# A two-layer decoder trunk on one core: block differences of the feed-forward's activations formed on VectorE when they are made, and product 2 summed in four PSUM banks

## The chip, the cores and the metric

The kernel runs on one core of one Trainium2 chip. The metric is the device time of one execution in microseconds; lower is better. TensorE (PE) multiplies into PSUM, VectorE (DVE), ScalarE (ACT) and GpSimd (POOL) work on SBUF and PSUM, and SyncE (SP) issues the transfers. PSUM has eight banks of [128, 512] f32 here, which the kernel deals out to two pools, A of three and B of five.

## The reference

Two layers on x of 1024 tokens by 1024 features, f32. Layer 0 mixes tokens with gated linear attention, layer 1 with differential attention; each is followed by a SwiGLU feed-forward, and a norm ends it. What the change touches is the feed-forward:

```python
def swiglu(h, w_in, w_out):
    gate, up = jnp.split(h @ w_in, 2, axis=-1)
    return (jax.nn.silu(gate) * up) @ w_out

for i in range(DEPTH):
    ...  # mixer of the layer: x = x + Mixer(rmsnorm(x))
    x = x + swiglu(rmsnorm(x, norm_ffn[i]), ffn_w_in[i], ffn_w_out[i])
return rmsnorm(x, norm_final)
```

w_in is 1024 x 5632 (gate and up of 2816 hidden features, 22 hidden tiles of 128), w_out is 2816 x 1024.

## The kernel before

Everything is kept transposed: features on the partitions, tokens along a row. The residual stream is eight row tiles of two token halves, `xt[k][s]`, each [128, 512] f32. A product of full precision is three matmuls: each operand is split into a high part (a cast on ScalarE, L143) and a low part (source minus high part, a subtraction on VectorE, L144), and high x high, high x low and low x high are summed in one bank. `split` does this for activations and weights; a matmul has 128x128 weights and 512 columns.

`swiglu` is called once per layer. `a` and `b` are its first and second token half. In its **first stage** it makes the 22 hidden tiles. Tiles 0 and 1 are computed directly; beside them the second token half's norm is finished and the sums and differences of normed blocks are made (`norm_b`, `combos`; `whole`, L925, adds a high and a low part together again). All other tiles go in seven block products (`p1` to `p7`, 12 matmuls each; Winograd's form of a 2x2 block product), in the order 2 to 18, 20, 21, 19. `finish` multiplies the up part by the gate and writes the result, [128, 512] of one token half, to DRAM (`stash`).

In the **second stage** the output products run over five groups of four hidden tiles. A group's activations are a 2x2 of blocks: B11 and B21 are token half a of the group's first and second pair of tiles, B12 and B22 the same of token half b. Their combinations T1 = B12 - B11, T3 = B22 - B12, T2 = B22 - T1, T4 = B21 - T2 and the blocks B11, B22, B21 enter seven products for each of four row pairs (rows i and i + 4). `oprod` does one of them (six matmuls) and adds the bank to one tile of the residual stream on VectorE (L881). Products 1, 6, 7, 4 of a row pair sum in one bank ("u"), 5 and 3 in another ("v"), 2 in a third ("w"); u is taken from pool B, v and w from pool A. The order of the products is a sorted list that sets them a few places apart:

```python
at = {1: 0, 5: 1, 6: 3, 3: 4, 2: 5, 7: 6, 4: 9}
order = sorted((7 * (4 * g + i) + at[n], g, i, n) for g in range(NG - 1) for i in range(4) for n in at)
```

`stash_steps(g)` makes the 20 steps that bring a group's blocks back: four loads of 512 KB (L804), the four differences on GpSimd (L818, 128x1024), and 14 splits. They are spread evenly beside the 28 products of the group before. `chunk_load` loads a row pair's weights (L828, 512 KB) and forms their four sums on GpSimd (L832 to L835, 128x256); `chunk` splits them. The last two hidden tiles, 20 and 21, have output products of their own (`direct_outp`, added at L916), with weights from `direct_weights` (L888) and activations from `direct_acts` (L906).

The **junction** lies between the stages: beside the products of tile 19 the first group's blocks and the first weights are loaded, differenced and split, and `direct_outp` for half a follows. The Tile framework keeps the order in which the code is written on each engine except where `tc.issue_after` or a priority moves it, and sets the semaphores; a tile's buffer is reused when its last reader is done.

Of the kernel before, what the change touches and what calls it, by code (L numbers as in the profile page):

```python
# [8 lines left out]
F32 = mybir.dt.float32  # L9
# [7 lines left out]
P = 128  # L17
# [9 lines left out]
NW = 5  # L27
# [27 lines left out]
def trunk_kernel(ctx: ExitStack, tc: tile.TileContext, xT, gin, gv, ga, gb, gout,  # L55
# [56 lines left out]
    # weights: two raw tiles and NW split sets, taken in turn  # L112
# [72 lines left out]
    def squares(s, ks, acc=None, c=slice(0, HT)):  # L185
        """Squares of rows ks, summed (on top of acc)."""
# [40 lines left out]
    def first_weights(layer, s):  # L227
        """Gate and up weights of the layer's first hidden tile, where token half s has left its normed tokens."""
# [12 lines left out]
    # ================= layer 0: gated linear attention =================  # L241
    pcA = ExitStack()
    psum(pcA, ("A", 3), ("B", 5))
    with ExitStack() as pc:
# [3 lines left out]
        def work():  # L248
            """Scratch; while the other token half's normed input is idle, its slots serve too."""
# [14 lines left out]
        def load_gate():  # L264
            # ga holds the 16 columns twice: the second copy becomes their low part
# [12 lines left out]
        # The tokens of the first half enter the projections before their norm's scale is known: it is a factor of  # L278
        # each token, and the results take it.
# [131 lines left out]
        def unit_steps(u):  # L411
# [23 lines left out]
            def level(m):  # L435
# [160 lines left out]
        # in the order in which tokens and weights come in  # L596
# [43 lines left out]
    # ================= SwiGLU =================  # L640
    # gate and up products of a hidden tile in seven block products (Winograd's form; rows: gate, up; contraction
    # halves; columns: the token halves). The first two hidden tiles go directly: their products hide the norm of
    # the second token half and the combinations of its blocks.
    def swiglu(layer, gcol, first_w, last, first=0):
# [5 lines left out]
        with ExitStack() as pc:  # L650
# [62 lines left out]
            def prod(ps, f, wn, bn, cont=False):  # L713
                """Block product into a bank; cont: on top of what the bank holds."""
# [53 lines left out]

            def finish(f, s, up, gate):
                g, r = divmod(f, 4)  # L770
                e = ftile(f"e{c.setdefault('e', 0) % 4}")
                c["e"] += 1
# [6 lines left out]
            stash = [dram.tile([P, 4096], F32, name=f"stash{layer}_{g}") for g in range(NG + 1)]  # L779
            X, SB = {}, {}  # L780
# [598 lines left out]
```

## Time and profile before

| | |
|---|---|
| median of 3 runs | 2437.61 us (2436.07 to 2438.44) |
| span of the profiled execution | 2436.8 us; no other time of its own is recorded |
| first mixer, to about | 498 us |
| feed-forward of layer 0: first stage, junction, groups | 498 to 920, 920 to 966, 966 to 1145 us |
| second mixer, to about | 1762 us |
| feed-forward of layer 1: first stage, junction, groups | 1762 to 2165, 2165 to 2219, 2219 to 2398 us |

Busy time of an engine over the span says which engine could bound the kernel; the list of waits says for which tile of which engine an engine stood still; the table of windows gives busy time, granted TensorE clock and DMA share of chosen stretches. The stages' bounds were read from the timeline.

### The profile page before, as it was taken

The numbers are of one execution on the slowest core, as the hardware profiler recorded it, in microseconds if no ns is written. First come the engines' busy times: TensorE is split into PE (matmuls) and PEld (weight loads), VectorE is DVE, ScalarE is ACT, GpSimd is POOL, SyncE is SP. The second block draws the span as 40 slices with busy tenths as digits, with TensorE's granted clock in tenths as the row PEclk, the third lists the DMA queues.
The fourth block names the chain that finished last, engine by engine and source line by source line (L and its number), as shares of the span: only waits on it lengthen the run. The fifth ranks groups of instructions, "written<-read, shape, count | busy, mean of one in ns | idle before, by whom it ended". The sixth has DMA issues, their size and how long they took to land. (4 is left out here: it accounts for less than half of the span.)

```text
span 2436.8 us, 31021 instructions
## 1 busy us (share of the span) xinstructions
PE 2363.2 (97%) x11930; PEld 1958.5 (80%) x11930; DVE 1814.3 (74%) x2890; ACT 1077.0 (44%) x1741; POOL 374.3 (15%) x284
## 2 busy tenths in 40 slices
PE   8999999999999998999999999999899999999997
PEld 6888888877888887787788878787678888877876
DVE  7767765887666559999876675857886655679998
ACT  6445644534333334334565454646443333333334
POOL 4000000030000004773000000000220000025763
PEclk9999999999999999999999999999999999999999
DMA  5122222113222223332010101010023222234322
GB/s 188 61 70 70 70 78 78 53 44 112 79 86 85 89 78 121 107 108 98 27 35 18 36 18 40 31 36 29 18 65 101 88 89 78 78 100 128 101 87 87
DMA packets 59780, 180.68 MB, mean 74 GB/s; under 512 B 6640, under 2 KB 8816, under 8 KB 59632
## 3 DMA queue, kind: packets, MB, share of 16 engines
q1 hardware_dynamic: 59344, 178.55, 22.7%
q8 instruction: 94, 1.54, 0.3%
q14 instruction: 54, 0.44, 0.1%
q10 hardware_dynamic: 288, 0.16, 0.0%
HBM read 151.41 MB, written 27.26 MB: 73 GB/s over the span
## 5 line engine op out<-in xcount | busy, mean ns | idle before, releaser
L925 POOL TENSOR_TENSOR t4h<-hh,hl 128x512 f32<-128x512 f32 x8 | 13.9, 1754 | 1037.5 <-DVE hl L144 1037.5
L832 POOL TENSOR_TENSOR sums<-wraw 128x256 f32<-128x256 f32 x40 | 32.2, 806 | 846.0 <-PE psB L718 368.8
L144 DVE TENSOR_TENSOR w3h<-wraw,w3h 128x512 fp32r<-128x512 f32 x40 | 27.7, 692 | 161.1 <-ACT w3h L143 161.1
L144 DVE TENSOR_TENSOR w0l<-wraw,w0h 128x1024 fp32r<-128x1024 f32 (+2 forms) x60 | 67.9, 1132 | 90.3 <-ACT w0h L143 90.2
L1149 ACT ACTIVATE p<-sp,mx 128x128 f32<-128x128 f32 (+7 forms) x128 | 94.8, 743 | 78.5 <-DVE mx L1146 77.9
L881 DVE TENSOR_TENSOR x<-x,psB 128x512 f32<-128x512 f32 (+1 forms) x180 | 119.2, 665 | 9.6 <-PE psB L879 8.6
L717 PE MATMUL psB<-hh,w0h 128*128 128x512 f32 x320 | 124.7, 390 | 0.3 <-ACT rs L726 0.2
L719 PE MATMUL psB<-hh,w0l 128*128 128x512 f32 x320 | 124.6, 389 | 0.0
L718 PE MATMUL psB<-hl,w0h 128*128 128x512 f32 x320 | 124.5, 389 | 0.0
L1145 DVE TENSOR_REDUCE mx<-sp 128x1 f32<-128x128 f32 (+7 forms) x128 | 94.9, 753 | 39.0 <-PE sp L1143 37.8
L143 ACT CAST w0h<-wraw 128x1024 fp32r<-128x1024 f32 (+2 forms) x60 | 58.8, 980 | 128.6 <-PE psB L718 98.4
L143 ACT CAST w2h<-wraw 128x1024 fp32r<-128x1024 f32 (+2 forms) x58 | 56.9, 980 | 114.4 <-PE psB L718 92.4
L225 DVE TENSOR_TENSOR x<-x,psA 128x512 f32<-128x512 f32 x108 | 73.5, 684 | 37.8 <-PE psA L150 35.8
L143 ACT CAST w3h<-wraw 128x512 fp32r<-128x512 f32 x42 | 26.1, 621 | 149.5 <-DMA wraw<-in_fin 145.6
L1174 PE MATMUL psO<-aT,vd 128*128 128x128 f32 x576 | 80.6, 280 | 0.5 <-ACT aT L1170 0.4
L1174 PEld LDWEIGHTS psO<-aT,vd 128*128 128x128 f32 x576 | 72.7, 192 | 9.3 <-ACT aT L1170 7.2
L1140 PE MATMUL sp<-kk,qh 128*128 128x512 f32 (+2 forms) x192 | 73.7, 384 | 5.1 <-DVE kk L1098 3.2
L143 ACT CAST w1h<-wraw 128x1024 fp32r<-128x1024 f32 (+1 forms) x44 | 45.5, 1035 | 60.1 <-DVE wraw L689 49.2
L881 DVE TENSOR_TENSOR x<-x,psA 128x512 f32<-128x512 f32 x104 | 69.2, 675 | 3.1 <-PE psA L879 2.7
L717 PEld LDWEIGHTS psB<-hh,w0h 128*128 128x128 f32 x320 | 60.1, 188 | 13.5 <-ACT rs L726 1.2
L717 PE MATMUL psB<-t3h,w2h 128*128 128x512 f32 x160 | 63.9, 399 | 7.0 <-DVE sq L744 7.0
L719 PEld LDWEIGHTS psB<-hh,w0l 128*128 128x128 f32 x320 | 60.1, 188 | 12.8 <-DVE w0l L144 0.3
(666 smaller groups left out, 8106.4 us busy)
## 6 DMA issues: line engine op xcount, KB each, us to landing
wraw<-in_fin SPq DMA_DIRECT2D x88, 512.0 KB, 3.9
stash<-e SPq DMA_DIRECT2D x88, 256.0 KB, 2.6
wraw<-in_foutc SPq DMA_DIRECT2D x40, 512.0 KB, 3.7
wraw<-in_gin SPq DMA_DIRECT2D x32, 512.0 KB, 3.7
raw<-stash SPq DMA_DIRECT2D x20, 512.0 KB, 4.5
wraw<-in_gv SPq DMA_DIRECT2D x16, 512.0 KB, 3.6
wraw<-in_gout SPq DMA_DIRECT2D x16, 512.0 KB, 3.6
wraw<-in_din SPq DMA_DIRECT2D x16, 512.0 KB, 3.6
```

The costliest lines, as they stand in the source:

```text
L143: ins = nc.scalar.copy(out=hi, in_=src)
L144: nc.vector.tensor_tensor(out=lo, in0=src, in1=hi.bitcast(F32), op=ALU.subtract)
L225: nc.vector.tensor_tensor(out=xt[m][s], in0=xt[m][s], in1=ps, op=ALU.add)
L717: mm(ps, ah, bh, start=s, stop=False, skip_group_check=cont)
L718: mm(ps, ah, bl, start=False, stop=False, skip_group_check=cont)
L719: mm(ps, al, bh, start=False, stop=i == KH - 1, skip_group_check=cont)
L832: op(out=s1, in0=a21, in1=a22, op=ALU.add)
L881: tt(out=xt[i + o][s][:, c], in0=xt[i + o][s][:, c], in1=ps, op=ALU.add)
L1140: mm(out, qh[:, o:o + P], kk[:, :w], start=True, stop=False)
L1145: nc.vector.reduce_max(out=mx, in_=sp[:, :W], axis=AX.X)
L1149: nc.scalar.activation(out=p[:, :W], in_=sp[:, :W], func=AF.Exp, scale=scale, bias=mx, accum_out=sm)
L1174: mm(c["op"][:, o:o + P], tl["v", n // 2][:, j, v * P:(v + 1) * P], aT[:, j * P:(j + 1) * P], start=j == 0, stop=j == i)
```

## The change

`finish` no longer writes only the four blocks. As soon as an activation is made, it also forms T1, T3, T2 and T4 from it on VectorE ([128, 512] each, 40 per layer), and the stash of a group holds seven blocks, in 14 pieces of 256 KB. `stash_steps` loads these straight into the tiles of the low parts and splits them in place: 14 steps where there were 20. B11 of group 0 is loaded and split early, beside tile 19's first products. The sums of `whole` and all combinations of normed blocks move from GpSimd to VectorE, those for T4 behind product 1. The sums of the first two weight chunks move to VectorE, the others stay. Product 2 of all five groups sums in the banks that `direct_outp` of half a has begun for rows 0 to 3 (`WB`: the three banks of pool A and one of B) and is added to the residual stream once, in the last group; u and v of all row pairs take turns in the other four banks of pool B.

```diff
+            def etile():
+                c["e"] = c.get("e", -1) + 1
+                return ftile(f"e{c['e'] % 4}")
+
+            def keep(g, o, t):
+                nc.sync.dma_start(out=stash[g][:, o * HT:(o + 1) * HT], in_=t)
+
             def finish(f, s, up, gate):
+
+
                 g, r = divmod(f, 4)
...
+                j = r % 2
+                d = blk.setdefault((g, j), {})
+                if g < NG and r < 2 and s == b:
+                    if ("keep", g) not in blk:
+                        blk["keep", g] = ftile("raw0", 1024), ftile("raw1", 1024)
+                    d["B12"], d["T1"] = [t[:, j * HT:(j + 1) * HT] for t in blk["keep", g]]
+                    e = d["B12"]
+                else:
+                    e = etile()
                 tt(out=e, in0=up, in1=gate, op=ALU.mult)
-                o = (r // 2 * 2 + (s == b)) * 1024 + r % 2 * HT
-                nc.sync.dma_start(out=stash[g][:, o:o + HT], in_=e)
...
+                if g == NG:
+                    return keep(g, 2 * (s == b) + j, e)
+                put = lambda n, t: keep(g, 2 * NAMES.index(n) + j, t)
+                if s == a:
+                    d["ea"] = e
+                    put("B21" if r > 1 else "B11", e)
+                elif r < 2:
+                    tt(out=d["T1"], in0=e, in1=d["ea"], op=ALU.subtract)
+                    put("T1", d["T1"])
+                else:
+                    put("B22", e)
+                    tt(out=d["B12"], in0=e, in1=d["B12"], op=ALU.subtract)
+                    put("T3", d["B12"])
+                    t2, t4 = etile(), etile()
+                    tt(out=t2, in0=e, in1=d["T1"], op=ALU.subtract)
+                    put("T2", t2)
+                    tt(out=t4, in0=d["ea"], in1=t2, op=ALU.subtract)
+                    put("T4", t4)
...
+            stash = [dram.tile([P, 7168 if g < NG else 2048], F32, name=f"stash{layer}_{g}") for g in range(NG + 1)]
+            NAMES = ("B11", "T1", "T2", "B22", "B21", "T3", "T4")
+            X, SB, blk = {}, {}, {}
...
                 if g % 2 == 0:
-                    t = ht(range(2, KD), a) + ft((2, 3))
-                    order = ("B11", "T3", "T2", "B22", "T1", "B21", "T4")
+                    w4 = [wpool.tile([P, 1024], F32R, name=f"w4{x}") for x in "hl"]
+                    t = ([[t[:, o:o + HT] for o in (0, HT)] for t in w4] + ht(range(2, 4), a) + ft((2,)) + ht(range(4, KD), a) +
+                         ft((3,))[:2])
                 else:
                     t = ht(range(KD), b) + ft((4,)) + ht(range(2), a)
-                    order = ("T2", "T3", "T4", "T1", "B22", "B21", "B11")
-                return {n: t[2 * i:2 * i + 2] for i, n in enumerate(order)}
+                return {n: t[2 * i:2 * i + 2] for i, n in enumerate(NAMES)}
...
+
+                def load(names):
+                    X.setdefault(g, {})
+                    for n in names:
+                        X[g][n] = X["slots", g][n]
+                        for j in range(2):
+                            o = (2 * NAMES.index(n) + j) * HT
+                            nc.sync.dma_start(out=X[g][n][j][1].bitcast(F32), in_=stash[g][:, o:o + HT])
 
                 def sp(n, j):
                     def go():
-                        split(*X[g][n][j], R[n][:, j * HT:(j + 1) * HT])
+                        hi, lo = X[g][n][j]
+                        split(hi, lo, lo.bitcast(F32))
...
-                def comb(n, x, y):
-                    # the result takes the place of an operand that is not needed again
-                    dst = {"T1": "B11", "T3": "B12", "T2": "B22", "T4": "B21"}[n]
-                    sub(out=R[dst], in0=R[x], in1=R[y], op=ALU.subtract)
-                    R[n] = R[dst]
+                def slot():
...
                 sps = lambda n: [lambda j=j: sp(n, j) for j in range(2)]
-                return ([load] + sps("B11") + [lambda: comb("T1", "B12", "B11")] + sps("B22") +
-                        [lambda: comb("T3", "B22", "B12"), lambda: comb("T2", "B22", "T1")] + sps("T1") +
-                        sps("B21") + sps("T2") + [lambda: comb("T4", "B21", "T2")] + sps("T3") + sps("T4"))
+                return load, slot, sum([sps(n) for n in NAMES], [])
...
-                op = nc.gpsimd.tensor_tensor
+                op = tt if (g, i) < (0, 2) else nc.gpsimd.tensor_tensor
...
-                cont = n not in (1, 5, 2)
-                if not cont:
-                    PB[g, i, bk] = bank(pools[bk])
+                cont = n not in (1, 5)
+                if n == 2:
+                    PB[g, i, bk] = WB[i]
+                    if g < NG - 1:
+                        tg = ()
+                elif not cont:
+                    PB[g, i, bk] = bank("B")
                 ps = PB[g, i, bk][:, c]
...
             def direct_outp(w, s, ms):
                 for m in ms:
-                    ps = bank()
+                    ps = bank("B" if s == a and m == 3 or s == a and m > 3 else "A")
                     o = m % 4 * P
                     for j, (hi, lo) in enumerate(w[m // 4]):
                         mm3(ps, hi[:, o:o + P], lo[:, o:o + P], *acts[4 * NG + j, s], j == 0, j == 1)
-                    tt(out=xt[m][s], in0=xt[m][s], in1=ps, op=ALU.add)
-
-            # ---- normed tokens of the second half, and the combinations of normed blocks ----
+                    if s == a and m < 4:
+                        WB[m] = ps
+                    else:
+                        tt(out=xt[m][s], in0=xt[m][s], in1=ps, op=ALU.add)
...
             def whole(t, k):
-                nc.gpsimd.tensor_tensor(out=t, in0=hh[k][a].bitcast(F32), in1=hl[k][a].bitcast(F32), op=ALU.add)
+                tt(out=t, in0=hh[k][a].bitcast(F32), in1=hl[k][a].bitcast(F32), op=ALU.add)
                 return t
...
             def norm_b():
-                with tc.issue_after(tmp_last["sq"]):
-                    c["t1"] = [whole(ftile(f"t4h{j}"), j) for j in JS]
-                    c["t4"] = [whole(ftile(f"t3l{j}"), KH + j) for j in JS]
...
             def combos():
-                t1, t2, t3, t4 = c["t1"], c["t2"], c["t3"], c["t4"]
+                t1 = c["t1"] = [whole(ftile(f"t4h{j}"), j) for j in JS]
+                t2, t3 = c["t2"], c["t3"]
                 for j in JS:
                     tt(out=t1[j], in0=t3[j], in1=t1[j], op=ALU.subtract)
-                    nc.gpsimd.tensor_tensor(out=t3[j], in0=t2[j], in1=t3[j], op=ALU.subtract)
+                    tt(out=t3[j], in0=t2[j], in1=t3[j], op=ALU.subtract)
                     tt(out=t2[j], in0=t2[j], in1=t1[j], op=ALU.subtract)
-                    nc.gpsimd.tensor_tensor(out=t4[j], in0=t4[j], in1=t2[j], op=ALU.subtract)
+
+            def combos4():
+                t2 = c["t2"]
+                t4 = c["t4"] = [whole(ftile(f"t3l{j}"), KH + j) for j in JS]
+                for j in JS:
+                    tt(out=t4[j], in0=t4[j], in1=t2[j], op=ALU.subtract)
...
             with tc.issue_after(tmp_last["p1"]):
+                combos4()
                 t_split(4)
...
                 if f == DFT - 3:
+                    load0, slot0, split0 = stash_steps(0)
+                    slot0()
+                    load0(NAMES[:1])
+                    emit(split0[:2])
                     direct_acts(a)
-                    s0 = stash_steps(0)
-                    s0[0]()
-                    c0 = chunk_load(0, 0)
                     wd = direct_weights(a)
                 p6(f)
                 p2(f)
                 for p in (p5, p7, p3) if f != DFT - 3 else (p7, p5, p3):
                     p(f)
+            load0(NAMES[1:])
+            c0 = chunk_load(0, 0)
+            direct_outp(wd, a, range(4))
             with tc.issue_after(tmp_last["p5"]):
+                emit(split0[2:4])
                 chunk(0, 0, c0)
-            emit(s0[1:12])
-            with tc.issue_after(tmp_last["p5"]):
-                direct_outp(wd, a, range(3))
-                emit(s0[12:])
-                direct_outp(wd, a, range(3, KD))
+                emit(split0[4:10])
+                direct_outp(wd, a, range(4, KD))
+                emit(split0[10:])
             chunk(0, 1)
             direct_acts(b)
...
                     if i == 0 and g < NG - 1:
                         emit(pend)
-                        pend = stash_steps(g + 1)
+                        load, slot, pend = stash_steps(g + 1)
+                        slot()
+                        load(NAMES)

...
-                oprod(g, i, n, {"u": "B", "v": "A", "w": "A"})
+                oprod(g, i, n)
                 if pend:
-                    done += 20
+                    done += 14
```

VectorE and GpSimd at the end of layer 0's mixer. Before, GpSimd has the eight sums of L925 (hh and hl are the high and low part of the first token half's normed tokens):

```order
L925 TENSOR_TENSOR t4h_4702<-hh_0_4257,hl_0_4258 128x512
L925 TENSOR_TENSOR t4h_4704<-hh_0_4263,hl_0_4264 128x512
L925 TENSOR_TENSOR t4h_4706<-hh_0_4269,hl_0_4270 128x512
L925 TENSOR_TENSOR t4h_4708<-hh_0_4275,hl_0_4276 128x512
L925 TENSOR_TENSOR t3l_4710<-hh_0_4281,hl_0_4282 128x512
L925 TENSOR_TENSOR t3l_4712<-hh_0_4287,hl_0_4288 128x512
L925 TENSOR_TENSOR t3l_4714<-hh_0_4293,hl_0_4294 128x512
L925 TENSOR_TENSOR t3l_4716<-hh_0_4299,hl_0_4300 128x512
```

In the changed kernel they stand on VectorE (L962 is the line in it), behind the last squares of the mixer and among the steps of the norm of the second token half (L181 to L183) and the first `finish` (L789):

```order
L191 TENSOR_TENSOR sqacc<-sqacc,sq 128x512
L962 TENSOR_TENSOR t4h_4891<-hh_0_4257,hl_0_4258 128x512
L962 TENSOR_TENSOR t4h_4893<-hh_0_4263,hl_0_4264 128x512
L962 TENSOR_TENSOR t4h_4895<-hh_0_4269,hl_0_4270 128x512
L962 TENSOR_TENSOR t4h_4897<-hh_0_4275,hl_0_4276 128x512
L962 TENSOR_TENSOR t3l_4987<-hh_0_4281,hl_0_4282 128x512
L962 TENSOR_TENSOR t3l_4989<-hh_0_4287,hl_0_4288 128x512
L181 SCALAR_TENSOR_TENSOR sq<-psA,t2l_4620 128x512
L962 TENSOR_TENSOR t3l_4991<-hh_0_4293,hl_0_4294 128x512
L182 SCALAR_TENSOR_TENSOR sq<-sq,t2l_4620 128x512
L789 TENSOR_TENSOR e_4748<-w3l,psB 128x512
L183 SCALAR_TENSOR_TENSOR t2l_4620<-sq,t2l_4620 128x512
L962 TENSOR_TENSOR t3l_4993<-hh_0_4299,hl_0_4300 128x512
```

What moved: GpSimd has nothing left at this place, and VectorE's rows ahead of the sums are those of before.

VectorE at the junction, behind the last `prep_up` of the first stage. Before (w4h, w4l and raw hold the blocks of group 0; the t4 splits are the weights of the last two hidden tiles; L744 adds product 6's bank, and frees it for product 7 of tile 19):

```order
L773 TENSOR_TENSOR e_7448<-sq 128x512
L144 TENSOR_TENSOR hl_0_7513<-w4h,hh_0_7512 128x512
L144 TENSOR_TENSOR hl_0_7515<-w4h,hh_0_7514 128x512
L144 TENSOR_TENSOR hl_0_7503<-hl_0_7503,hh_0_7502 128x512
L144 TENSOR_TENSOR t2l_7525<-raw_7543,t2h_7524 128x512
L144 TENSOR_TENSOR t4l_7558<-wraw,t4h_7557 128x512
L144 TENSOR_TENSOR t4l_7562<-wraw,t4h_7561 128x512
L744 TENSOR_TENSOR sq<-rs,psB 128x512
L144 TENSOR_TENSOR hl_0_7508<-hl_0_7508,hh_0_7507 128x512
L144 TENSOR_TENSOR t2l_7527<-raw_7543,t2h_7526 128x512
L144 TENSOR_TENSOR t2l_7529<-w4h,t2h_7528 128x512
```

In the changed kernel:

```order
L789 TENSOR_TENSOR e_7530<-sq 128x512
L144 TENSOR_TENSOR t4l_7633<-wraw,t4h_7632 128x512
L144 TENSOR_TENSOR hl_0_7621<-hl_0_7621,hh_0_7620 128x512
L144 TENSOR_TENSOR t4l_7637<-wraw,t4h_7636 128x512
L144 TENSOR_TENSOR hl_0_7626<-hl_0_7626,hh_0_7625 128x512
L744 TENSOR_TENSOR sq<-rs,psB 128x512
L144 TENSOR_TENSOR t4l_7643<-wraw,t4h_7642 128x512
L144 TENSOR_TENSOR t4l_7647<-wraw,t4h_7646 128x512
L757 TENSOR_TENSOR sq<-rs,psB 128x512
L758 TENSOR_TENSOR rs<-sq,psB 128x512
L789 TENSOR_TENSOR e_7694<-rs,w3l 128x512
L766 TENSOR_TENSOR sq<-sq,sqacc 128x512
```

What moved: four splits of blocks of group 0 left their place ahead of L744 or just behind it, and the direct activations' splits (hl_0_7621, hl_0_7626) came there; the rest of group 0 is split later.

SyncE's queue at the same place. Before, the four loads of group 0's blocks stand far ahead of these rows, which hold the first chunk's weights (L828), the direct tiles' puts, loads and weights, and the first load of group 1 (stash_1):

```order
L828 DMA wraw<-in_foutc 128x1024
L775 DMA stash_5_4557<-e_7430 128x512
L906 DMA hl_0_7503<-stash_5_4557 128x512
L888 DMA wraw<-in_foutd 128x1024
L775 DMA stash_5_4557<-e_7448 128x512
L906 DMA hl_0_7508<-stash_5_4557 128x512
L906 DMA e_7775<-stash_5_4557 128x512
L888 DMA wraw<-in_foutd 128x1024
L804 DMA w4h<-stash_1_4553 128x1024
L828 DMA wraw<-in_foutc 128x1024
```

In the changed kernel, from the first weights of the direct tiles on (L774 puts, L938 loads the direct activations, L835 the blocks; hl_0_7587 and hl_0_7589 are T1, the t2l tiles T2 and B22):

```order
L920 DMA wraw<-in_foutd 128x1024
L774 DMA stash_5_4557<-e_7512 128x512
L938 DMA hl_0_7621<-stash_5_4557 128x512
L835 DMA hl_0_7587<-stash_0_4552 128x512
L835 DMA hl_0_7589<-stash_0_4552 128x512
L774 DMA stash_5_4557<-e_7530 128x512
L938 DMA hl_0_7626<-stash_5_4557 128x512
L920 DMA wraw<-in_foutd 128x1024
L835 DMA t2l_7591<-stash_0_4552 128x512
L835 DMA t2l_7593<-stash_0_4552 128x512
L835 DMA t2l_7595<-stash_0_4552 128x512
L835 DMA t2l_7597<-stash_0_4552 128x512
```

What moved: group 0's blocks but for B11 (two loads, far ahead still) and T1 are now ten loads of 256 KB behind the last weights of the direct tiles, six more than shown, with the first two weight chunks behind them; each goes into a tile that the products of tile 19 read before.

## Rows read from the trace of the kernel before

**Rows 1.** The page: busy time, share of the span, instructions.

```profile
PE 2363.2 (97%) x11930; PEld 1958.5 (80%) x11930; DVE 1814.3 (74%) x2890; ACT 1077.0 (44%) x1741; POOL 374.3 (15%) x284
```

**Rows 2.** TensorE's waits: total us, times, longest.

```profile
PE psB L717 <- DVE sq L744: 7.0, 2, 3.5
PE psB L877 <- DVE x L881: 6.9, 13, 1.0
PE psB L173 <- DVE sqacc L549: 5.3, 1, 5.3
PE psA L148 <- DVE x L916: 4.2, 2, 2.2
...
PE psA L148 <- DVE x L225: 2.4, 2, 1.9
...
PE sp L148 <- DVE x L225: 2.2, 1, 2.2
...
PE psB L717 <- ACT w1h L143: 1.5, 2, 0.7
...
PE psB L719 <- DVE w1l L144: 1.0, 2, 0.5
```

**Rows 3.** Timeline at the end of layer 0's mixer: start, us, instruction [idle before].

```profile
486.97 5.05 POOL L925 TENSOR_TENSOR t4h<-hh,hl 128x512 f32<-128x512 f32 x3 [5.67 <-DVE hl L144]
...
487.38 3.49 DVE L205 SCALAR_TENSOR_TENSOR sq<-x,vec,rs 128x512 f32<-128x512 f32 x2
...
491.39 2.86 DVE L144 TENSOR_TENSOR hl<-sq,hh 128x512 fp32r<-128x512 f32 x2
...
497.74 1.19 PE L173 MATMUL psB<-sqacc,ones 128*128 128x512 f32 x1 [5.33 <-DVE sqacc L549]
```

**Rows 4.** Timeline at the end of layer 1's mixer, VectorE.

```profile
1748.11 3.46 DVE L205 SCALAR_TENSOR_TENSOR sq<-x,vec,rs 128x512 f32<-128x512 f32 x2
```

**Rows 5.** Timeline of layer 0's junction.

```profile
927.73 2.90 DVE L144 TENSOR_TENSOR t2l<-raw,t2h 128x512 fp32r<-128x512 f32 x1
...
933.93 0.67 DVE L744 TENSOR_TENSOR sq<-rs,psB 128x512 f32<-128x512 f32 x1
...
934.65 0.72 PE L717 MATMUL psB<-t3h,w2h 128*128 128x512 f32 x1 [3.52 <-DVE sq L744]
```

**Rows 6.** Windows: us, busy per engine, granted clock, DMA share, GB/s.

```profile
560.00:920.00 360.00, 359.32 (x1584) 296.89 (x1583) 222.65 (x295) 121.14 (x164) 0.00 (x0) 1.00 0.28 89
966.00:1145.00 179.00, 176.10 (x768) 142.86 (x767) 171.73 (x236) 71.72 (x111) 115.52 (x84) 1.00 0.30 97
494.40:501.30 6.90, 3.56 (x7) 2.18 (x8) 6.68 (x7) 1.32 (x2) 4.31 (x3) 0.51 0.00 0
934.80:938.20 3.40, 3.40 (x9) 2.62 (x10) 3.40 (x4) 1.11 (x2) 2.22 (x1) 0.50 0.51 159
1747.10:1750.50 3.40, 3.40 (x8) 2.73 (x9) 3.40 (x4) 1.14 (x2) 2.83 (x2) 0.50 0.00 0
```

**Rows 7.** VectorE's groups, first stage: busy, mean ns, idle before.

```profile
L773 DVE TENSOR_TENSOR e<-rs,w3l 128x512 f32<-128x512 f32 x18 | 12.5, 692 | 0.6
```

**Rows 8.** DMA issues: KB each, us to landing.

```profile
raw<-stash SPq DMA_DIRECT2D x20, 512.0 KB, 4.5
...
hl<-stash SPq DMA_DIRECT2D x4, 256.0 KB, 4.1
```

**Rows 9.** Timeline, VectorE, second half's norm in layer 0.

```profile
524.93 0.69 DVE L181 SCALAR_TENSOR_TENSOR sq<-psA,t2l 128x512 f32<-128x512 f32 x1 [3.44 <-ACT t2l L180]
```

**Rows 10.** VectorE's groups of layer 0's output products.

```profile
L881 DVE TENSOR_TENSOR x<-x,psB 128x512 f32<-128x512 f32 x78 | 52.6, 677 | 3.6 <-PE psB L879 3.2
...
L144 DVE TENSOR_TENSOR hl<-raw,hh 128x512 fp32r<-128x512 f32 x12 | 14.9, 1239 | 0.0
L144 DVE TENSOR_TENSOR w1l<-sums,w1h 128x1024 fp32r<-128x1024 f32 x7 | 14.3, 2050 | 0.9 <-ACT w1h L143 0.9
L144 DVE TENSOR_TENSOR w3l<-sums,w3h 128x1024 fp32r<-128x1024 f32 x7 | 8.5, 1219 | 0.9 <-ACT w3h L143 0.9
```

More of the change, by code (lines that the diff above doesn't have):

```diff
@@ L767, in p3 @@
                 finish(f, b, d["u3"], d["u2"])
+            def etile():
[3 more added lines that the diff above has]
+                nc.sync.dma_start(out=stash[g][:, o * HT:(o + 1) * HT], in_=t)
             def finish(f, s, up, gate):
                 g, r = divmod(f, 4)
-                e = ftile(f"e{c.setdefault('e', 0) % 4}")
-                c["e"] += 1
-                tt(out=e, in0=up, in1=gate, op=ALU.mult)
-                o = (r // 2 * 2 + (s == b)) * 1024 + r % 2 * HT
-                nc.sync.dma_start(out=stash[g][:, o:o + HT], in_=e)
-            stash = [dram.tile([P, 4096], F32, name=f"stash{layer}_{g}") for g in range(NG + 1)]
-            X, SB = {}, {}
+                j = r % 2
[7 more added lines that the diff above has]
+                    e = etile()
+                tt(out=e, in0=up, in1=gate, op=ALU.mult)
+                if g == NG:
[19 more added lines that the diff above has]
+            X, SB, blk = {}, {}, {}
             def slots(g):
@@ L786, in slots @@
                 if g % 2 == 0:
-                    t = ht(range(2, KD), a) + ft((2, 3))
-                    order = ("B11", "T3", "T2", "B22", "T1", "B21", "T4")
+                    w4 = [wpool.tile([P, 1024], F32R, name=f"w4{x}") for x in "hl"]
+                    t = ([[t[:, o:o + HT] for o in (0, HT)] for t in w4] + ht(range(2, 4), a) + ft((2,)) + ht(range(4, KD), a) +
+                         ft((3,))[:2])
                 else:
                     t = ht(range(KD), b) + ft((4,)) + ht(range(2), a)
-                    order = ("T2", "T3", "T4", "T1", "B22", "B21", "B11")
-                return {n: t[2 * i:2 * i + 2] for i, n in enumerate(order)}
+                return {n: t[2 * i:2 * i + 2] for i, n in enumerate(NAMES)}
             def stash_steps(g):
-                R = {}
-                sub = nc.gpsimd.tensor_tensor
-                def load():
-                    X[g] = slots(g)
-                    R.update(zip(("B11", "B12", "B21", "B22"),
-                                 [wpool.tile([P, 1024], F32, name=f"w4{x}") for x in "hl"] +
-                                 [ftile(f"raw{i}", 1024) for i in range(2)]))
-                    for i, n in enumerate(("B11", "B12", "B21", "B22")):
-                        nc.sync.dma_start(out=R[n], in_=stash[g][:, i * 1024:(i + 1) * 1024])
+                def load(names):
[5 more added lines that the diff above has]
+                            nc.sync.dma_start(out=X[g][n][j][1].bitcast(F32), in_=stash[g][:, o:o + HT])
                 def sp(n, j):
                     def go():
-                        split(*X[g][n][j], R[n][:, j * HT:(j + 1) * HT])
+                        hi, lo = X[g][n][j]
+                        split(hi, lo, lo.bitcast(F32))
                     if g == 0:
@@ L866, in swiglu, with oprod @@
             PB = {}
-            def oprod(g, i, n, pools, c=slice(0, HT)):
+            def oprod(g, i, n, c=slice(0, HT)):
                 wn, xn, bk, tg = PR[n]
-                cont = n not in (1, 5, 2)
-                if not cont:
-                    PB[g, i, bk] = bank(pools[bk])
+                cont = n not in (1, 5)
[5 more added lines that the diff above has]
+                    PB[g, i, bk] = bank("B")
                 ps = PB[g, i, bk][:, c]
@@ L908, in direct_acts @@
                     acts[4 * NG + j, s] = hi, lo
+            WB = {}
             def direct_outp(w, s, ms):
                 for m in ms:
-                    ps = bank()
+                    ps = bank("B" if s == a and m == 3 or s == a and m > 3 else "A")
                     o = m % 4 * P
@@ L1046, in swiglu @@
                 last(lambda: direct_outp(wd, b, range(KD)),
-                     lambda n, *c: [oprod(NG - 1, i, n, {"v": "B"}, *c) for i in range(4)])
+                     lambda n, *c: [oprod(NG - 1, i, n, *c) for i in range(4)])
     def to_attention(direct, blocks):
```

1 line of the change is left out of this document (added).

## Prediction

> **What bounds the kernel now.** I read the list of busy times first: TensorE (PE) is busy in 97% of the span, VectorE (DVE) in 74% [rows 1]. So only a wait of TensorE, or a stretch in which its clock is low, can be won. The list of what TensorE waited for comes next [rows 2], and then, for each of those places, the timeline. The reader is to see that the waits that touch this change lie in five places of each layer's feed-forward or just ahead of it, and that nearly all have VectorE as releaser.
>
> At each, the timeline shows the same thing: while GpSimd runs a subtraction or addition whose operands lie in SBUF, VectorE's own operations with two SBUF operands take 1.2 to 2.9 us instead of 0.68. In the end of layer 0's mixer two VectorE scalings take 3.49 us and two subtractions 2.86 us beside the eight GpSimd sums of L925, so that the squares on which TensorE waits come 5.33 us late [rows 3]. In the end of layer 1's mixer it is the same picture [rows 4]. At the junction between the two feed-forward stages one subtraction takes 2.90 us beside the L818 differences, and L744, which frees a bank, comes 3.52 us late [rows 5]. Operations with one operand in PSUM are not slowed (0.67 us for L744 there).
>
> A second loss lies behind these waits. The granted clock is 1.00 in steady work, where a matmul comes every 360/1584 = 0.227 us. In stretches of 3.4 to 6.9 us that follow a wait it is 0.50 (1.2 in place of 2.4 GHz), and a matmul comes every 3.40/8 = 0.425 us [rows 6]. I count seven such stretches beside the places of the change: one at the end of the first mixer, two at the end of the second (the shown one and one at 1757.4), two at each junction (934.8 and 951.8, and the same in layer 1). Work done at half clock costs 1 - 0.227/0.425 = 0.465 of its own time, so 3.40 x 0.465 = 1.58 us for each short one and 3.56 x 0.465 = 1.65 us for the long one, of whose 6.9 us TensorE worked 3.56.
>
> **The change, part by part.**
>
> *Differences formed as activations are made.* It adds 40 VectorE subtractions of 128x512 per layer. The product beside them, of that size and two SBUF operands, takes 692 ns [rows 7]: 40 x 0.69 = 27.6 us. They fall into the first stage of the feed-forward, where VectorE is busy 222.65 of 360 us, without GpSimd, and TensorE 359.32 of 360 [rows 6]. That idle 137 us hides them; without this cover they would be 55 us in two layers. Each is queued ahead of a product's read of its bank by at most three such subtractions (2.1 us); a product takes 12 x 0.227 = 2.7 us, and banks B are five, so I take 0.
>
> The Trainium skill ("Perfetto Trace Analysis", section Optimizing Scalar/DVE Operations) says to move work off a saturated VectorE, to GpSimd even, but adds that the two share a read port, so that this might not help. By its first half the change goes the wrong way, since VectorE is busy 171.73 of 179 us in the groups; the rows say that work of this kind leaves the groups and does not enter them, and that the price of having it on GpSimd shows on VectorE.
>
> *Seven blocks loaded in place of four.* 14 loads of 256 KB per group instead of 4 of 512 KB. Loads of 256 KB land after 4.1 us, those of 512 KB after 4.5 [rows 8]. For groups 1 to 4 they are issued a group (some 36 us) ahead: 0. For group 0 they are not; that is the junction, below.
>
> *Term 1, end of layer 0's mixer.* The L925 sums leave GpSimd, and VectorE's order up to them is unchanged. Its operations go back to 0.68, the two pairs of [rows 3] alone win 3.49 + 2.86 - 4 x 0.68 = 3.6 us, and the L549 sum then needs only its ScalarE cast. I take 0.3 of the 5.3 us wait as left, and the half clock with its 1.65 us as gone: **-6.6** (bounds -5.0, if the clock falls anyway, and -6.9). The eight sums now stand on VectorE behind it, 8 x 0.69 = 5.5 us. VectorE waits 3.44 us there for a ScalarE result [rows 9]; so at most 2.1 us are late, onto the second half's normed tokens, which the first direct tiles' products (12 us and more) cover: 0.
>
> *Term 2, end of layer 1's mixer.* Waits of 2.4 and 2.2 us on L225 [rows 2], and two half-clock stretches. I leave 0.5 of the waits: -4.1 - 3.2 = **-7.3** (bounds -4.1 and -7.8).
>
> *Term 3, first block products.* The waits on w1h and w1l, 1.5 and 1.0 us [rows 2], come from weight splits queued behind combinations that ran beside GpSimd's. The T4 combination now comes later, after product 1: **-2.5** (bounds 0 and -2.5).
>
> *Term 4, junctions.* Now: 7.0 us on L744 and 4.2 us on L916 in the two layers [rows 2], and four half-clock stretches, 6.3: 17.5 together. GpSimd does none of this any more, so L744 comes in time. What is late next: the blocks of group 0. Their tiles come free only as tile 19's products end; product 7 stands ready at 934.65 - 3.52 = 931.1 [rows 5], so product 2 before it began at 928.4, and only from there can T2 and B22 be loaded. Ten blocks and a weight chunk are 3.0 MB; the stretch with 159 GB/s at a DMA share of 0.51 [rows 6] scales to 312 GB/s, so 9.6 us: 938 to 940, the weight chunk last. TensorE meanwhile has products 7, 5 and 3 (8.2 us) and four direct products of six matmuls (5.4 us): to 944.7. The chunk needs four sums on VectorE (128x256, some 0.4 us each, half of 0.69 and a bit), two casts and two subtractions on ScalarE and VectorE (up to 1.2 us each, as w3l in [rows 10], casts alike): 6 us, to 945 or 946. The second chunk stands behind it with as much work, while the first pair's products last 9.5 us. So I take 1 to 2 us of wait on the first and 2.5 to 3.5 on the second chunk or the late blocks: 4.5 us per layer, 9.0 in all, without half clock. **-8.5** (bounds -17.5, all in time; 0, the late loads bring waits as long as those removed).
>
> *Term 5, groups.* 16 adds per layer of product 2 go, and 4 direct ones: 20 x 0.677 = 13.5 us of 171.73. Of the splits beside GpSimd, 12 at 1239 ns and 7 at 2050 ns [rows 10] fall to about 0.69 and 1.22 for the greater part, as the 512-wide and the other 1024-wide ones have it: 12.4 us more. VectorE then stands near 146 of 179 us at best, and its adds that free banks come sooner. Of the 6.9 us on L881 [rows 2] I leave 1.4, because the chunk sums stay on GpSimd: **-5.5** (bounds -6.9; and +4, 0.1 us for each of 40 row pairs, since four banks now turn for products 1 and 5).
>
> Sum: -6.6 - 7.3 - 2.5 - 8.5 - 5.5 = -30.4 us. The profiled execution has only its span, 2436.8; the median of the runs is 2437.6, 0.8 above, which I take as its surroundings. 2437.6 - 30.4 = **2407**. All good ends give 2396, all bad ends 2432.5.
>
> **Rivals.**
>
> *A late junction.* If the block loads and VectorE's chunk sums bring back waits as long as the old ones, term 4 is 0: 2416. For it: 3.0 MB in one burst, one queue, ahead of work that is due at once. Against it: 13.6 us of product work before the first need.
>
> *A clear junction.* Everything is in time: 2407 - 9 = 2398.
>
> *Slower: banks.* Products 1, 6, 7, 4 of a row pair hold one bank, 5 and 3 another, and all pairs now turn in four, where five and three served before. If TensorE waits for a bank in each of the 40 row pairs, the change turns slower at 30.4/40 = 0.76 us per pair; at 1.0 us, the longest of the present L881 waits [rows 2], the time is 2437.6 - 30.4 + 40 = 2447. Against it: in the steady order a row pair takes seven products, the first bank lives ten, the second four, so no more than three are held at a time, and one add of 0.68 us fits into a product of 1.36.
> The Trainium skill ("Perfetto Trace Analysis", section Matmul Optimizations) wants all eight banks in use to give instructions more freedom; here all eight are in use still, but four only to hold sums. No run here yet shows such a wait.
>
> *The change doesn't do what it says.* VectorE's slowness beside GpSimd has another cause, or the same waits go to VectorE's longer queue: 2433 to 2442.
>
> **How the numbers follow.** Chances: the forecast 0.55, late junction 0.25, clear junction 0.08, banks 0.07, no effect 0.05. The forecast's own range is 2401 to 2413; to leave out no more than 2 in 10 the range reaches from the clear junction to beyond the late one: 2398 to 2424. Faster by over 0.2% (4.9 us, about what a measurement here can tell) 0.87, within it 0.06, slower 0.07.
>
> **What would show it.** Right: no L549 wait above 1 us before 498 and clock 1.00 there; VectorE's L205 and L144 at 0.68 us at the ends of both mixers; no L744 wait; first-stage TensorE still without idle time; L881's successor with under 3 us. Wrong: waits on sums, splits or block loads of over 9 us per layer after the junction, with half clock behind them, or waits for a bank at each row pair.

## The result and the profile after

The changed kernel takes 2403.74 us (median of 4 runs, 2401.89 to 2404.05) where the kernel before took 2438.03 beside it: ratio 0.9857, 95% interval 0.9844 to 0.987. That is 34.3 us less. The forecast was 2407, with a range of 2398 to 2424.

The page of the changed kernel, busy times (answers to [rows 1]):

```profile
span 2400.1 us, 31300 instructions
...
PE 2350.9 (98%) x11930; PEld 1951.0 (81%) x11930; DVE 1792.0 (75%) x2978; ACT 1076.1 (45%) x1741; POOL 191.8 (8%) x196
```

TensorE's work is the same 11930 matmuls; its busy time falls by 12.3 us because less of it runs at half clock; the rest of the gain is waits. What TensorE waited for, whole run: total us, times, longest (answers to [rows 2]):

```profile
PE psB L909 <- DVE x L913: 4.4, 6, 1.4
...
PE psB L911 <- DVE w2l L144: 1.3, 2, 0.7
...
PE psB L717 <- DVE sq L744: 1.1, 1, 1.1
...
PE psB L909 <- DVE x L953: 0.4, 1, 0.4
...
PE psB L173 <- DVE sqacc L549: 0.2, 1, 0.2
```

L225, L916 (now L953) and the waits on w1h and w1l are gone or below 0.5 us; L744 is left with 1.1 in one layer. VectorE and TensorE at the end of layer 0's mixer, timeline (answers to [rows 3]):

```profile
485.92 1.41 DVE L205 SCALAR_TENSOR_TENSOR sq<-x,vec,rs 128x512 f32<-128x512 f32 x2
487.25 0.68 DVE L225 TENSOR_TENSOR x<-x,psA 128x512 f32<-128x512 f32 x1
487.85 1.29 DVE L144 TENSOR_TENSOR hl<-sq,hh 128x512 fp32r<-128x512 f32 x2
...
491.45 1.10 PE L173 MATMUL psB<-sqacc,ones 128*128 128x512 f32 x2 [0.16 <-DVE sqacc L549]
```

The pair of L205 takes 1.41 us, not 3.49, the pair of L144 1.29, not 2.86, and the wait of 5.33 us is 0.16. The end of layer 1's mixer (answers to [rows 4]):

```profile
1725.00 1.41 DVE L205 SCALAR_TENSOR_TENSOR sq<-x,vec,rs 128x512 f32<-128x512 f32 x2
```

Windows of the changed kernel (answers to [rows 6]; us, busy time of PE, PEld, DVE, ACT and POOL, granted clock, DMA share, GB/s): the end of the mixer with the start of the feed-forward, the first stage, the junction, the groups.

```profile
491.00:552.00 61.00, 60.84 (x263) 49.03 (x262) 59.22 (x92) 26.98 (x42) 0.00 (x0) 1.00 0.17 58
550.00:910.00 360.00, 360.00 (x1590) 298.10 (x1589) 247.06 (x332) 120.11 (x162) 0.00 (x0) 1.00 0.31 103
905.00:950.00 45.00, 43.83 (x190) 34.91 (x189) 36.73 (x59) 21.50 (x35) 0.59 (x1) 1.00 0.84 285
950.00:1128.00 178.00, 175.16 (x763) 142.03 (x762) 153.48 (x225) 72.58 (x112) 73.02 (x72) 1.00 0.39 125
```

The granted clock is 1.00 at all of these. The first stage holds 24 us more VectorE work and TensorE has no idle time in it. At the junction the DMA share is 0.84: the late loads are there, and TensorE still works 43.8 of 45 us.

To place the gain I took the start of the same matmul in both traces (TensorE's order is the same but for the second stage) and noted how far ahead the changed kernel is:

| stretch | gained there, us | forecast |
|---|---|---|
| ahead of any changed work (at 45 us) | 1.0 | 0 |
| term 1, end of layer 0's mixer | 7.0 | 6.6 |
| term 2, end of layer 1's mixer | 7.6 | 7.3 |
| term 3, first block products, two layers | 2.05 + 2.35 | 2.5 |
| terms 4 and 5, junction, groups and end, two layers | 9.05 + 8.5 | 14.0 |
| second mixer elsewhere | -1.0 | 0 |

They add up to 36.5 of the 36.7 us between the two spans.

### The profile page after: what moved, and what is told of

It is laid out like the page before. It is cut to its first block, busy times and chain, and to the rows that moved or that the text cites. A ratio compares the mean times of both kernels' runs of the same rounds, so it can differ in the third digit from the quotient of the medians.

```text
span 2400.1 us, 31300 instructions
## 1 busy us (share of the span) xinstructions
PE 2350.9 (98%) x11930; PEld 1951.0 (81%) x11930; DVE 1792.0 (75%) x2978; ACT 1076.1 (45%) x1741; POOL 191.8 (8%) x196
## 5 line engine op out<-in xcount | busy, mean ns | idle before, releaser
L913 DVE TENSOR_TENSOR x<-x,psB 128x512 f32<-128x512 f32 (+1 forms) x246 | 162.8, 670 | 32.8 <-PE psB L911 32.5
L144 DVE TENSOR_TENSOR w0l<-wraw,w0h 128x1024 fp32r<-128x1024 f32 (+2 forms) x60 | 68.2, 1137 | 90.6 <-ACT w0h L143 90.6
L144 DVE TENSOR_TENSOR w3h<-wraw,w3h 128x512 fp32r<-128x512 f32 x40 | 27.7, 692 | 110.0 <-ACT w3h L143 110.0
L225 DVE TENSOR_TENSOR x<-x,psA 128x512 f32<-128x512 f32 x108 | 73.5, 684 | 37.5 <-PE psA L150 35.5
L718 PEld LDWEIGHTS psB<-hl,w0h 128*128 128x128 f32 x320 | 60.1, 188 | 12.5
L144 DVE TENSOR_TENSOR w2l<-wraw,w2h 128x1024 fp32r<-128x1024 f32 (+2 forms) x58 | 66.3, 1143 | 0.3
L1187 PE MATMUL sp<-kk,ql 128*128 128x512 f32 (+2 forms) x192 | 65.8, 354 | 0.0
```

The lines of the kernel that those rows point to most:

```text
L144: nc.vector.tensor_tensor(out=lo, in0=src, in1=hi.bitcast(F32), op=ALU.subtract)
L225: nc.vector.tensor_tensor(out=xt[m][s], in0=xt[m][s], in1=ps, op=ALU.add)
L718: mm(ps, ah, bl, start=False, stop=False, skip_group_check=cont)
L913: tt(out=xt[i + o][s][:, c], in0=xt[i + o][s][:, c], in1=ps, op=ALU.add)
L1187: mm(out, qlo[:, o:o + P], kk[:, :w], start=False, stop=not lastb)
```

## The experiments

My theory: what costs time in the kernel before is GpSimd reading SBUF beside VectorE's operations with two SBUF operands, at the few places where TensorE waits for VectorE. Rivals: the order or amount of VectorE's work there; the banks; any activity of GpSimd. All runs but the last three were measured beside the kernel before, but not beside the changed kernel; I set them against its 2403.74 us, and since it took 2402.65 in the last three, and the kernel before 2436.0 to 2438.0 throughout, such a difference has 1 to 2 us of doubt.

**The norm's part alone.** The kernel before, with `whole` and the combinations as the changed kernel has them:

```diff
-                nc.gpsimd.tensor_tensor(out=t, in0=hh[k][a].bitcast(F32), in1=hl[k][a].bitcast(F32), op=ALU.add)
+                tt(out=t, in0=hh[k][a].bitcast(F32), in1=hl[k][a].bitcast(F32), op=ALU.add)
...
-                    nc.gpsimd.tensor_tensor(out=t3[j], in0=t2[j], in1=t3[j], op=ALU.subtract)
+                    tt(out=t3[j], in0=t2[j], in1=t3[j], op=ALU.subtract)
```

> The kernel before, with only the sums of whole and the combinations of normed blocks on VectorE (T4's behind product 1); block differences, loads and banks as before. My theory: the waits at the ends of both mixers and at the first block products come from GpSimd sums beside VectorE's own operations, so this part alone takes what the two traces show at these places, 7.0 + 6.6 + 4.4 = 18 us: 2420 us (the recorded terms 1 to 3 say 16.4: 2421). L549 and L225 waits under 1 us, clock 1.00 at 494 us; the junction and the groups keep all their waits. Rival, the waits only go elsewhere because VectorE has 16 operations more per layer: less than 8 us gained.

Measured: 2418.35 us, ratio 0.9922 (0.9908 to 0.9937), 19.4 us gained. The L549 and L225 waits are gone; L744 stays at 7.0 us, and L881 has 7.7 (6.9 before). Terms 1 to 3 are this part, and it needs none of the others. Over half of the change is here.

**GpSimd's sums put back as extra work.** The changed kernel, with the eight sums again on GpSimd, read by nobody:

```diff
             def norm_b():
+                with tc.issue_after(tmp_last["sq"]):
+                    for k in range(KD):
+                        x = ftile(f"t4h{k}" if k < KH else f"t3l{k - KH}")
+                        nc.gpsimd.tensor_tensor(out=x, in0=hh[k][a].bitcast(F32), in1=hl[k][a].bitcast(F32), op=ALU.add)
```

> The changed kernel, with the eight sums of 128x512 put back on GpSimd at the ends of both mixers as extra work whose result nobody reads (VectorE still makes its own). My theory: VectorE's L205 and L144 take 1.2 to 1.8 us each again beside them, the waits on L549 (about 5 us) and L225 (about 4.6 us) and the low clock come back: 2403.7 + 12 to 14 = 2416 to 2418 us. Rival, the gain came from the order or number of VectorE's operations there: no change, 2402 to 2406 us.

Measured: 2416.68 us (0.9915, 0.99 to 0.993). VectorE's timeline at the end of layer 0's mixer, and the list of TensorE's waits:

```profile
488.54 3.48 DVE L205 SCALAR_TENSOR_TENSOR sq<-x,vec,rs 128x512 f32<-128x512 f32 x2
491.95 0.68 DVE L225 TENSOR_TENSOR x<-x,psA 128x512 f32<-128x512 f32 x1
492.55 2.87 DVE L144 TENSOR_TENSOR hl<-sq,hh 128x512 fp32r<-128x512 f32 x2
```

```profile
PE psB L173 <- DVE sqacc L549: 5.3, 1, 5.3
...
PE psA L148 <- DVE x L225: 4.0, 2, 2.1
```

In layer 1 it is the same:

```profile
1734.10 3.46 DVE L205 SCALAR_TENSOR_TENSOR sq<-x,vec,rs 128x512 f32<-128x512 f32 x2
```

The durations of before return to within 0.01 us, with VectorE's own list untouched, and a granted clock of 0.50 returns behind them (498.2 to 505.0 us). L225, which has one operand in PSUM, stays at 0.68. The order or number of VectorE's operations is ruled out as the cause at these two places; the run does not reach the junction.

**GpSimd writes in place of reads.**

```diff
+                        nc.gpsimd.tensor_tensor(out=x[:, :8], in0=hh[k][a].bitcast(F32)[:, :8],
+                                                in1=hl[k][a].bitcast(F32)[:, :8], op=ALU.add)
+                        for r in range(3):
+                            nc.gpsimd.memset(x, float(r))
```

> The changed kernel, with extra GpSimd work at the same places that writes SBUF and hardly reads it: for each of the eight tiles one sum of 8 columns (to tie it to the same moment) and three memsets of 128x512. If only GpSimd operations that read SBUF slow VectorE: VectorE's L205 and L144 stay at 0.68 us, 2402 to 2405 us. If any GpSimd access of SBUF does: as with the sums, L549 and L225 waits of several us, up to 2418 us.

Measured: 2401.1 us (0.9852, 0.9835 to 0.9868), no loss. GpSimd's and VectorE's timelines in it:

```profile
489.39 5.67 POOL L980 MEMSET t4h<- 128x512 f32 x12
495.00 5.70 POOL L980 MEMSET t3l<- 128x512 f32 x12
```

```profile
490.65 0.69 DVE L549 TENSOR_TENSOR sqacc<-sqacc,sq 128x512 f32<-128x512 f32 x1 [0.22 <-ACT sq L548]
...
492.52 1.22 DVE L139 TENSOR_TENSOR w2l<-wraw,w2h 128x1024 fp32r<-128x1024 f32 x1
```

Two-operand operations keep their time beside memsets. The memsets came only as the mixer's last L205 and L144 were done, so they meet other lines than expected (L549, L139), also with two SBUF operands. So the sign that I named, L205 and L144 at 0.68 us beside them, was not tested; these others were. The Trainium skill ("SBUF — State Buffer", section SBUF: two separate sides) says that a VectorE operation with two SBUF inputs contends only with a GpSimd operation that reads SBUF, and that one of the two then waits; this and the run before agree, with 0.69 and 1.44 us for such an operation (2.87 the pair).

**First chunks' sums back on GpSimd.**

```diff
-                op = tt if (g, i) < (0, 2) else nc.gpsimd.tensor_tensor
+                op = nc.gpsimd.tensor_tensor
```

> The changed kernel, with the sums of the first two weight chunks on GpSimd too. My theory: at the junction the four sums take 4 to 5 us in place of 1.7, and VectorE's splits beside them slow down; the second chunk, for which TensorE waits 0.6 to 0.7 us now, comes 2 to 4 us later, in both layers: 2407 to 2412 us. Rival, the eight direct products of half a cover it: 2403 to 2405 us.

Measured: 2410.51 us (0.989, 0.9875 to 0.9905): 6.8 us slower. The wait is not where I expected it: 7.1 us in all on L953 (0.4 in the changed kernel), the direct products' adds that free product 1's bank; those on L913 grow from 4.4 to 6.3 us, and the one on the second chunk's split is gone. VectorE's timeline shows them at the end of its queue, behind a split that waits and differences that run slow:

```profile
937.06 1.22 DVE L144 TENSOR_TENSOR w1l<-sums,w1h 128x1024 fp32r<-128x1024 f32 x1 [1.92 <-ACT w1h L143]
...
941.11 1.22 DVE L804 TENSOR_TENSOR e<-e,raw 128x512 f32<-128x512 f32 x1
...
945.81 1.87 DVE L953 TENSOR_TENSOR x<-x,psB 128x512 f32<-128x512 f32 x3
```

**Product 2 added in every group, banks as before.**

```diff
+                cont = n not in (1, 5, 2)
+                if not cont:
+                    PB[g, i, bk] = bank(pools[bk])
...
+                    ps = bank()
```

> The changed kernel, with product 2 not summed over the groups: its own bank in pool A each time and an add to the residual stream after each, 5 and 3 in pool A, 1, 6, 7, 4 in pool B, as before. VectorE gets 20 adds more per layer, 13.5 us, and has 178 - 153.5 = 24 us idle in the groups. My theory (the sums matter little now that GpSimd no longer slows VectorE): 2403 to 2407 us against 2403.7. Recorded term 5 (adds and contention, -5.5 together) would put it at 2406 to 2409. Rival, that the four circulating banks make the waits of 4.4 us on L913: these go, 2400 to 2402 us.

Measured: 2409.99 us (0.9891, 0.9875 to 0.9908), 6.3 above the changed kernel and more than I expected. The waits by stretch, layer 0: junction (905 to 975 us, the three longest), then groups (975 to 1135 us):

```profile
PE psA L148 <- DVE x L946: 2.2, 2, 1.4
PE psB L907 <- DVE w2l L144: 1.7, 1, 1.7
PE psB L905 <- DVE x L909: 0.8, 1, 0.8
```

```profile
PE psB L905 <- DVE x L909: 1.4, 2, 1.2
PE psB L905 <- ACT w3h L143: 0.6, 1, 0.6
```

Layer 0's groups lose nothing by 16 more adds: 2.0 us of waits, against 2.6 in the changed kernel there; layer 1's have 2.8 against 1.7. Most of the loss lies at the junction, where the eight direct products again share three banks and VectorE has four adds more; which of the two costs the time, this run does not separate. So the sums in PSUM pay, but there. The rival that four circulating banks cost TensorE falls too: the waits on product adds do not go away (4.4 us on L909, which is L913 in the changed kernel).

**Differences on GpSimd, where they are now.**

```diff
-                    tt(out=d["T1"], in0=e, in1=d["ea"], op=ALU.subtract)
+                    nc.gpsimd.tensor_tensor(out=d["T1"], in0=e, in1=d["ea"], op=ALU.subtract)
```

and so for T3, T2 and T4.

> The changed kernel, with the 40 block differences per layer formed where they are now, in the first stage, but on GpSimd. My theory: it is the place that counts. GpSimd is busy some 40 x 1.5 = 60 us per layer in the first stage, VectorE's operations with two SBUF operands take up to 1.2 us beside it, and its idle time there (113 of 360 us) hides that: first stage without TensorE waits. Only the last differences, at the junction, cost 1 to 3 us per layer: 2406 to 2410 us. Rival, GpSimd beside VectorE costs wherever it runs: TensorE waits in the first stage, over 2415 us.

Measured: 2415.16 us (0.9911, 0.9896 to 0.9925), 11.4 above, with its four runs 7 us apart. The median is outside the range of my theory and just in that of its rival, but by the windows the first stage is as my theory has it, and the junction is worse than its price. Windows of the first stage, and GpSimd's timeline at the junction:

```profile
555.00:915.00 360.00, 360.00 (x1590) 298.08 (x1589) 225.03 (x296) 120.46 (x163) 45.28 (x36) 1.00 0.32 106
```

```profile
936.32 4.69 POOL L801 TENSOR_TENSOR raw<-e,raw 128x512 f32<-128x512 f32 x1 [55.39 <-DVE e L789]
940.96 1.84 POOL L804 TENSOR_TENSOR e<-e,raw 128x512 f32<-128x512 f32 x1
942.88 1.62 POOL L806 TENSOR_TENSOR e<-e,e 128x512 f32<-128x512 f32 x1
```

Where VectorE has gaps, GpSimd's 45 us cost TensorE nothing. At the junction VectorE has none, and now it is GpSimd's operation that takes 4.69 us. The puts (writes to DRAM) that wait for it hold up SyncE's queue and the loads behind them: the direct activations' load goes out 8.7 us after the put of the last activation (936.27, then 944.94), where in the changed kernel it is 3.4 us (934.53, then 937.95). ScalarE's cast stands behind such a load, and TensorE waits 8.0 us in all, in two layers, for w3h.

**Other chunk sums on VectorE: all, or those of the last group.**

```diff
-                op = tt if (g, i) < (0, 2) else nc.gpsimd.tensor_tensor
+                op = tt
...
+                op = tt if (g, i) < (0, 2) or g == NG - 1 else nc.gpsimd.tensor_tensor
```

> The changed kernel, with the sums of all weight chunks on VectorE, so that GpSimd does nothing in the groups. Each chunk's four sums are 1.7 us there; 18 chunks more per layer are 30 us, of which about 6 come back as contention: VectorE at some 172 to 177 of 178 us in the groups. If contention and the wait for GpSimd's results are what is left of waits: the waits of 1.4 us at the last group's first products go, 2400 to 2402 us. If VectorE's own load counts: adds come late, over 2406 us.

> The changed kernel, with the four chunk sums of the last group too on VectorE (the first two were there already). The trace after shows at its first products a wait of 1.40 us in each layer, on an add that stands behind a VectorE split which waits for a ScalarE cast, which waits for GpSimd's sums of the chunk (4,1). My theory: both waits go, 2403.7 - 2 to 3 = 2400.5 to 2401.7 us. Rival, it is the bank order: no change.

Measured: 2397.84 us with all (0.9841, 0.9826 to 0.9856), 2398.85 with the last group's (0.9846, 0.9831 to 0.986). The windows of the groups, all on VectorE and then the last group's:

```profile
950.00:1128.00 178.00, 177.45 (x780) 145.95 (x780) 174.00 (x299) 70.60 (x112) 0.00 (x0) 1.00 0.38 122
```

```profile
950.00:1128.00 178.00, 177.77 (x779) 145.44 (x780) 159.38 (x244) 72.03 (x112) 58.53 (x56) 1.00 0.38 125
```

TensorE goes from 175.16 to 177.5 us and more of 178. VectorE at 174 of 178 us still does not hold TensorE up here. Both times are a little below what I expected. Since the last group's sums give all of it but 1 us, which is within the runs' spread, the waits were those of the last group's products. Whether GpSimd's sums caused them by taking longer or by slowing VectorE, these runs do not separate.

**The cover of the junction.**

```diff
                 emit(split0[4:10])
-                direct_outp(wd, a, range(4, KD))
                 emit(split0[10:])
...
+                if (g, i, n) == (0, 1, 1):
+                    direct_outp(wd, a, range(4, KD))
                 oprod(g, i, n)
```

> The changed kernel, with the four direct products of half a for rows 4 to 7 moved from ahead of the first row pair to behind its first products. Recorded term 4 counted only the four for rows 0 to 3 as cover of the group 0 loads and first chunks; the trace after has all eight ahead of product 1, 5.4 us more. If that miscount is why the junction waits are 2.8 us in place of 9.0: 3 to 4.5 us of waits per layer on the first two chunks' splits and the blocks' come back, 2408 to 2412 us. Rival, loads and splits come in time anyway: 2402 to 2405 us.

> The changed kernel itself, on the same chip as the other runs of this call: 2402 to 2405 us.

> The changed kernel with all chunk sums on VectorE, again, beside the changed kernel on one chip: 4 to 7 us below it.

Measured on one chip: 2411.16 us with the cover moved (0.99, 0.9885 to 0.9915), 2402.65 for the changed kernel (0.986, 0.9844 to 0.9877), 2397.68 with all sums on VectorE (0.9842, 0.9827 to 0.9857). TensorE's waits at the two junctions with the cover moved:

```profile
PE psB L909 <- DVE x L913: 3.1, 1, 3.1
PE psA L911 <- DVE w2l L144: 1.2, 1, 1.2
```

```profile
PE psB L909 <- DVE x L913: 5.1, 1, 5.1
PE psA L911 <- DVE w2l L144: 1.2, 1, 1.2
```

4.3 us in layer 0 and 6.3 in layer 1: about the size that was forecast for the changed kernel, but the waiting is for an add (L913, product 1's) in VectorE's queue more than for the chunk's splits. The add stands behind the splits of the second half's direct activations, which wait 0.91 us in layer 0 and 2.97 in layer 1 for a ScalarE cast, and this for a load of `stash`. The low clock follows both waits (0.52 from 951 to 958 us). The trace is that of the slowest of the four runs, 4.3 us above their median, so its waits may be longer than usual. The edit also puts the four direct products into the banks that the first row pairs take turns in, so it moves more than cover. The kernel with all sums on VectorE has the lowest median both times, 5.0 us under the changed kernel here; all its runs lie below all of the changed kernel's (2399.88 at most, 2401.87 at least), but the two intervals overlap, and by the prediction 0.2% (4.9 us) is what a measurement here can tell.

## Why the prediction was right, and where its sizes were off

*Terms 1 and 2* (6.6 and 7.3 forecast, 7.0 and 7.6 measured) held in place, cause and size; extra sums on GpSimd alone bring back 12.9 us.

*Term 3* was too small: 2.5 for 4.4. The waits of 2.5 us in the list were removed, and the same matmuls came 1.9 us earlier besides; that rest stays open.

*Term 4* was mis-sized: 8.5 forecast. Of the 17.5 us before, 2.8 are left (0.4 + 0.7 in layer 0, 1.1 + 0.6 in layer 1), so 14.7 are gained. The chunk landed when forecast: 938 to 940 in times of before is 928 to 930 at the 10 us that the changed kernel is ahead there, and its first sum runs at 929.26. The step that failed is "four direct products of six matmuls": in the changed order all eight stand ahead of product 1, which starts at 940.66, and that is 5.4 us more cover. The moved cover bears this out in size (8.5 us lost), though not by the waits that were forecast. The chunk's work was put too high as well: from its first sum to its last split ahead of product 1 it took 4.6 us (929.26 to 933.90), not 6, so by these times the first chunk would have been ready with four direct products too. The rival that the junction would come late falls.

What took the waits on L744 away is not separated. Before, the splits ahead of it ran slow beside GpSimd's differences:

```profile
925.44 1.22 DVE L144 TENSOR_TENSOR hl<-w4h,hh 128x512 fp32r<-128x512 f32 x1
926.59 1.22 DVE L144 TENSOR_TENSOR hl<-hl,hh 128x512 fp32r<-128x512 f32 x1
...
930.55 3.45 DVE L144 TENSOR_TENSOR t4l<-wraw,t4h 128x512 fp32r<-128x512 f32 x2
```

With the split of 2.90 us in [rows 5] these are five in 8.5 us, where two such splits take 1.29 us in the changed kernel. But the change also moved splits of group 0's blocks out of this place, two of these five among them, about 4 us. By these rows either could be worth the 3.5 us wait, and no run changes one without the other.

*Term 5* was mis-sized the other way: 1.4 us of waits were to be left, 4.4 are, and about 2.5 are gained in place of 5.5. The reason given for what stays was right (chunk sums still on GpSimd), its price was not: in each layer one wait of 1.4 us falls at the last group's first products, and layer 0 has one of 0.9 near that group's end (1127.77); putting that group's sums on VectorE takes them away. The adds saved in the groups, a part of this term, are worth about nothing there; at the junction, where I had not counted them, fewer adds and the banks together are worth most of 6 us.

Terms 4 and 5 together are 14.0 forecast and 17.2 by these waits (17.55 by the start times). By the start times the five terms gained 36.55 us, 6.15 more than the 30.4 forecast. The medians show only 3.3 us of that (2407 against 2403.74), in part because the profiled execution was the fastest of its four, 1.85 us below their median. That the total came so close is in part luck: term 4 was 6.2 us too small and term 5 3.0 us too large. *Hidden at no cost*, as forecast: the 40 differences per layer, and the eight sums behind the mixer.

## What to carry to other kernels

Look at what GpSimd does beside the VectorE operation that a busy TensorE waits for, not at either engine's total: in this kernel, work that reads SBUF on GpSimd was dear where VectorE had no gaps (12.9 us for eight sums at the end of each mixer) and free where it had them (the differences in the first stage). Work can also be moved in time instead of between engines: the differences cost nothing on VectorE in an earlier stage where it idles, though no run shows this part of the gain by itself. At a junction between stages count everything that the order puts ahead of the first need, and every add, put or cast that stands in one queue with the late piece.

## What was not expected of the hardware

The slowing goes both ways: a GpSimd subtraction of 128x512 that takes 1.29 us in the first stage took 4.69 us beside a VectorE queue without gaps, and four VectorE splits beside it kept their pace:

```profile
936.16 2.49 DVE L144 TENSOR_TENSOR t2l<-t2l,t2h 128x512 fp32r<-128x512 f32 x4
```

And GpSimd's memsets, 0.47 us each for 128x512 (5.67 for 12), did not lengthen VectorE's operations with two SBUF operands, which stayed at 0.69 us.
